# The recurrent block of a hybrid diffusion step: GpSimd's work given to VectorE and ScalarE, layer 0's conditioning given to TensorE

## The chip, the cores and the metric

The kernel runs on one core of a Trainium2 chip. A core has TensorE (matrix products, PE in the profile, its weight loads PEld), VectorE (DVE), ScalarE (ACT), GpSimd (POOL) and a queue for transfers, SyncE (SP). The metric is the device time of one execution in microseconds (us).

## The reference, cut to what matters

1,024 latent tokens and 128 context tokens of width 1024 go through two layers. Layer 0 mixes tokens with a bidirectional RG-LRU, layer 1 with latent attention; each is followed by an MLP with a hidden width of 4096. Every sub-layer is normalised and modulated by six vectors a layer (shift, scale, gate, twice), which come from a conditioning vector, one for the latents and one for the context:

```
mod = silu(cond) @ w_ada + b_ada            # 1024 -> 6 x 1024, for c and c_ctx
sh1, sc1, g1, sh2, sc2, g2 = split(mod, 6)
h = rms_norm(x, g) * (1 + sc1) + sh1
```

The recurrent block of layer 0:

```
xb, yb = split(h @ w_in, 2);  yb = gelu(yb)
xb = depthwise_conv(xb, conv_w, conv_b)     # four taps along the tokens
r, i = sigmoid(xb @ wa + ba), sigmoid(xb @ wx + bx)   # 8 blocks of 128, two directions
a = exp(-8 * r * softplus(-lam));  b = sqrt(1 - a*a) * (i * xb)
h_t = a_t * h_(t-1) + b_t                   # forwards and backwards
out = ((h_f + h_b) * yb) @ w_out
x = x + g1 * out
```

## The kernel before

Channels lie on the 128 partitions and tokens along the row, 1,152 in three chunks of 384 (`CH`). Each float32 operand of a large product is split into two parts, hi and lo, and a product is three TensorE instructions (`mm3`, L118: hi hi, hi lo, lo hi), so a group of 8 blocks of k for one output tile and one chunk is 24 instructions into one of eight PSUM banks.

Weights come as a stream of pieces of 128x1024. `prefetch` (L83) loads a piece through SP into one of two `raw` buffers, ScalarE copies it to `whi` (L94) and GpSimd subtracts to get `wlo` (L95). The first 20 pieces (`RG_STREAM`) belong to the recurrent block.

The conditioning is done in two ways. For the first two vectors of layer 0 (j = 0 the shift, j = 1 the scale), `first_half` loads `ada_w0` and multiplies with the conditioning as the stationary operand (L420), which gives rows; the rows are copied and transposed back (L443, L446). The last four tiles of the scale are dot products instead: `ada_dot` (L142) on VectorE for the latents, and for the context a product on GpSimd (L435) that ScalarE sums later. All other tiles are dots: `ada` (L149) loads a 128x1024 tile of the transposed weights into a `raw` buffer and VectorE makes two dots (L144), one for each condition, against `cb`, the activated condition on every partition. Sixteen such tiles are taken during the recurrent block (`ADA_RG`), eight in its output projection, and the others in the MLP of layer 0.

After the norm of chunk 0 the first group makes x channels 0 and 1 and y channel 0 together for all chunks. Then `rglru` (L510) goes through n = 0 to 7 in the order `RG_ORDER`: the products of x channel n+1 (`xb`, L603), two or more chunks of y products (drained through Gelu, L599), and `gates(n)` (L540). ScalarE copies x out of PSUM (`copy_raw`, L516). `conv` (L519) makes the first tap with bias on GpSimd (L522) and adds three taps on VectorE, each in two segments (L529, six instructions). `conv_split` splits it (L138 on ScalarE, L139 on VectorE). `gates` does 36 products, twelve tanh passes (L554), exp (L563), tanh (L568), the product (L571), 1-A on GpSimd (L574), square root (L577), two products (L580, L581) and two scans for each direction (L585). GpSimd copies the final state (L589), adds both directions (L590) and multiplies with y (`finish`, L593). Row buffers of 128x1152 come from one pool of twelve (`unit`, L507); `raw_x` and `xf` of the convolution, `xfh`, `xfl`, `tr`, `ti`, `A` are all of it. At the end `hs` is split into `zhi`, `zlo`, and `rg_out` (L655) loads `cb` again from a copy in DRAM and starts the output projection.

The order on each engine is written by a scheduler from the program's order, and within an engine it is kept.

Of the kernel before, what the change touches and what calls it, by code (L numbers as in the profile page):

```python
# [15 lines left out]
D = 1024  # L16
# [35 lines left out]
ADA_ORDER = [(0, 2), (0, 3), (0, 4), (0, 5)] + [(1, _j) for _j in range(6)]  # L52

ADA_RG = (2, 2, 2, 2, 2, 2, 2, 2)


class Emit:
# [25 lines left out]
    def prefetch(self, upto):  # L83
# [3 lines left out]
        while self.piece_i < min(upto, self.I["wts"].shape[0]):  # L87
# [7 lines left out]
            nc.gpsimd.tensor_tensor(out=lo, in0=raw, in1=hi.bitcast(F32), op=ALU.subtract)  # L95
# [66 lines left out]
    def mod_finish(self, l, j, conds=(0, 1)):  # L162
# [100 lines left out]
    def group(self, items, rhs, drain, after=None, chunks=range(NCH)):  # L263
        """items: (m, piece index, [block of k]); rhs(k, c): (hi, lo)."""
# [72 lines left out]
    def run(self, stop=99):  # L337
        nc, tc, I, O = self.nc, self.tc, self.I, self.O
        with (
# [12 lines left out]
            self.one_row = const.tile([1, 128], F32, name="one_row")  # L352
            nc.vector.memset(self.one_row, 1.0)
# [5 lines left out]
            self.cb_d = nc.dram_tensor("cb_d", [1, 2, 1024], F32).ap()  # L359
# [13 lines left out]
    def make_cb(self, pool):  # L373
        nc = self.nc
        self.cb = pool.tile([128, 2, 1024], F32, name="cb")
        for i in range(2):
            row = self.wp.tile([128, 1024], F32, tag="raw", name="raw", bufs=2)[0:1]
            nc.sync.dma_start(row, self.I["crow"][:, i])
            for j in range(2):
                ps = self.bank(512)  # L380
                nc.tensor.matmul(
                    ps, lhsT=self.one_row, rhs=row[:, j * 512:(j + 1) * 512], start=True, stop=True
                )
                nc.scalar.activation(out=self.cb[:, i, j * 512:(j + 1) * 512], in_=ps, func=AF.Silu)

    def first_half(self, stop):
        nc, tc, I = self.nc, self.tc, self.I
        cbp = self.alloc(name="cb", bufs=1, side="right")
        rgt = self.alloc(name="rgt", bufs=1, side="right")
        self.cells = None  # L390
        self.junk = rgt.tile([128, 1024], mybir.dt.bfloat16, name="junk")
        self.rgt = rgt
        cs = self.rgt.tile([128, 2, 8], F32, name="cs")
        nc.scalar.activation(out=cs, in_=self.v("cond", 0, 16), func=AF.Silu)
        self.make_cb(cbp)
# [17 lines left out]
        row = [self.bank(512) for _ in range(3)]  # L413
        for k in range(8):
            if k % 2 == 0:
                w2 = self.cpool.tile([128, 2, 3, 512], F32, tag="C", name="ada0")
            w = w2[:, k % 2]
            nc.sync.dma_start(w, I["ada_w0"][k * 128:(k + 1) * 128].rearrange("p (i n) -> p i n", i=3))
            for i in range(3):
                nc.tensor.matmul(  # L420
                    row[i][0:2], lhsT=cs[:, :, k], rhs=w[:, i], start=(k == 0), stop=(k == 7)
                )
# [18 lines left out]
        for i in range(3):  # L441
            srow = self.unit("srow")[0:2, :512]
            tc.keep_in_program_order(nc.scalar.copy(out=srow, in_=row[i][0:2]))  # L443
            for k in range(4):
                o = 2 * (4 * i + k)
                nc.tensor.transpose(psm[:, o:o + 2], srow[:, k * 128:(k + 1) * 128], self.ident[0:2, 0:2])  # L446
        psm = psm.rearrange("p (k t) -> p t k", t=2)
# [62 lines left out]
    def rglru(self, H, gens):  # L510
# [97 lines left out]
        for n in range(2):  # L608
            raws[n] = self.unit("raw_x")
# [614 lines left out]
```

## Time and profile before

| | |
|---|---|
| time, median of 3 runs | 2902.98 us (2900.94 to 2904.37) |
| span of the profiled execution | 2905.1 us |
| TensorE busy | 2744.2 us, 94% of the span, 16,031 instructions |
| VectorE busy | 1483.3 us, 51% |
| ScalarE busy | 1142.5 us, 39% |
| GpSimd busy | 694.9 us, 24%, 337 instructions |
| mean granted TensorE clock | 0.969 |

The span runs from the first to the last instruction of one execution; no time of its own is listed for that execution beyond it, and the span is 2.1 us above the median of the runs. "Busy" is the time in which an engine works on an instruction. Idle time before an instruction is put down to what released it, after an arrow. The granted clock is TensorE's, as a share of 2.4 GHz; its two levels are 2.4 and 1.2 GHz, so 0.86 is a mean over time at both.

### The profile page before, as it was taken

The numbers are of one execution on the slowest core, as the hardware profiler recorded it, in microseconds if no ns is written. First come the engines' busy times: TensorE is split into PE (matmuls) and PEld (weight loads), VectorE is DVE, ScalarE is ACT, GpSimd is POOL, SyncE is SP. The second block draws the span as 40 slices with busy tenths as digits, with TensorE's granted clock in tenths as the row PEclk, the third lists the DMA queues.
The fourth block names the chain that finished last, engine by engine and source line by source line (L and its number), as shares of the span: only waits on it lengthen the run. The fifth ranks groups of instructions, "written<-read, shape, count | busy, mean of one in ns | idle before, by whom it ended". The sixth has DMA issues, their size and how long they took to land. (4 is left out here: it accounts for less than half of the span.)

```text
span 2905.1 us, 39768 instructions
## 1 busy us (share of the span) xinstructions
PE 2744.2 (94%) x16031; PEld 2700.1 (93%) x16031; DVE 1483.3 (51%) x2805; ACT 1142.5 (39%) x2174; POOL 694.9 (24%) x337
## 2 busy tenths in 40 slices
PE   7878679899999999998997999999999999999998
PEld 4878669899999999998997999999999999999998
DVE  7799986844354435326364666662732222223225
ACT  4555551422312322233334877872423222312332
POOL 4276662221211112122142000001211121212121
PEclk8989879999999999999998999999999999999999
DMA  5111114122222223112146211225011010101111
GB/s 220 44 58 59 58 51 174 58 95 80 80 95 70 97 67 106 61 59 102 40 131 224 77 55 56 75 75 191 30 37 51 30 59 30 59 30 51 37 43 67
DMA packets 78608, 223.89 MB, mean 77 GB/s; under 512 B 7764, under 2 KB 36244, under 8 KB 76758
## 3 DMA queue, kind: packets, MB, share of 16 engines
q1 hardware_dynamic: 77654, 218.19, 22.0%
q0 software_dynamic: 768, 3.15, 0.3%
q8 instruction: 126, 2.06, 0.3%
q14 instruction: 60, 0.48, 0.1%
HBM read 185.48 MB, written 33.21 MB: 75 GB/s over the span
## 5 line engine op out<-in xcount | busy, mean ns | idle before, releaser
L95 POOL TENSOR_TENSOR wlo<-raw,whi 128x1024 fp32r<-128x1024 f32 x181 | 454.2, 2510 | 1766.6 <-ACT whi L94 1742.3
L120 PE MATMUL ps<-hhi,whi 128*128 128x384 f32 x2088 | 706.4, 340 | 13.4 <-ACT hhi L247 9.5
L124 PE MATMUL ps<-hhi,wlo 128*128 128x384 f32 x2088 | 706.5, 339 | 4.1 <-POOL wlo L95 4.1
L123 PE MATMUL ps<-hlo,whi 128*128 128x384 f32 x2088 | 707.0, 339 | 0.0
L94 ACT CAST whi<-raw 128x1024 fp32r<-128x1024 f32 x181 | 190.3, 1052 | 868.7 <-PE ps L123 692.4
L120 PE MATMUL ps<-hid,whi 128*128 128x384 f32 x1536 | 516.2, 336 | 0.0
L123 PE MATMUL ps<-hid,whi 128*128 128x384 f32 x1536 | 515.5, 336 | 0.0
L124 PE MATMUL ps<-hid,wlo 128*128 128x384 f32 x1536 | 515.4, 336 | 0.0
L257 DVE SCALAR_TENSOR_TENSOR X<-ps,mod,X 128x256 f32<-128x256 f32 (+1 forms) x576 | 279.9, 514 | 446.2 <-PE ps L124 418.4
L120 PEld LDWEIGHTS ps<-hhi,whi 128*128 128x128 f32 x2088 | 397.7, 191 | 14.0 <-ACT hhi L247 9.6
L124 PEld LDWEIGHTS ps<-hhi,wlo 128*128 128x128 f32 x2088 | 397.7, 191 | 4.9 <-POOL wlo L95 4.9
L123 PEld LDWEIGHTS ps<-hlo,whi 128*128 128x128 f32 x2088 | 398.0, 191 | 0.5 <-DVE hlo L248 0.4
L139 DVE TENSOR_TENSOR hid<-cell,hid 128x384 fp32r<-128x384 f32 x192 | 138.8, 730 | 464.6 <-ACT hid L138 464.5
L120 PEld LDWEIGHTS ps<-hid,whi 128*128 128x128 f32 x1536 | 288.8, 188 | 0.0
L123 PEld LDWEIGHTS ps<-hid,whi 128*128 128x128 f32 x1536 | 288.7, 188 | 0.0
L124 PEld LDWEIGHTS ps<-hid,wlo 128*128 128x128 f32 x1536 | 288.7, 188 | 0.0
L144 DVE SCALAR_TENSOR_TENSOR junk<-raw,cb 128x1024 bf16<-128x1024 f32 x80 | 123.9, 1549 | 181.2 <-DMA raw<-ada_wt 172.1
L312 ACT ACTIVATE cell<-ps 128x384 f32<-128x384 f32 x192 | 93.6, 488 | 296.6 <-PE ps L124 296.4
L947 ACT ACTIVATE p<-ps,nm 128x384 f32<-128x384 f32 (+1 forms) x200 | 112.9, 576 | 39.9 <-DVE nm L942 39.8
L139 DVE TENSOR_TENSOR pt<-ps,pt 128x384 fp32r<-128x384 f32 (+1 forms) x200 | 106.5, 543 | 37.1 <-ACT pt L138 36.8
L932 DVE TENSOR_REDUCE mx<-ps 128x1 f32<-128x384 f32 (+1 forms) x200 | 108.0, 540 | 27.2 <-PE ps L931 26.5
L187 POOL TENSOR_TENSOR acc<-acc,cell 128x384 f32<-128x384 f32 x48 | 53.1, 1105 | 222.8 <-ACT cell L185 185.5
(188 smaller groups left out, 4327.0 us busy)
## 6 DMA issues: line engine op xcount, KB each, us to landing
raw<-wts SPq DMA_DIRECT2D x181, 512.0 KB, 3.7
raw<-ada_wt SPq DMA_DIRECT2D x80, 512.0 KB, 3.7
qn_d<-qn SPq DMA_DIRECT2D x12, 768.0 KB, 5.7
q<-qn_d SPq DMA_DIRECT2D x16, 576.0 KB, 4.5
o_d<-o SPq DMA_DIRECT2D x64, 128.0 KB, 1.7
ada<-ada_w SPq DMA_DIRECT2D x8, 768.0 KB, 12.1
x<-xt SPq DMA_DIRECT2D x3, 1536.0 KB, 10.8
X<-xt SPq DMA_DIRECT2D x3, 1536.0 KB, 11.2
```

Of the source, the lines that this page charges most:

```text
L94: nc.scalar.copy(out=hi, in_=raw)
L95: nc.gpsimd.tensor_tensor(out=lo, in0=raw, in1=hi.bitcast(F32), op=ALU.subtract)
L120: mm = nc.tensor.matmul(ps, lhsT=w[0], rhs=h[0], start=first, stop=False)
L123: nc.tensor.matmul(ps, lhsT=w[0], rhs=h[1], start=False, stop=False)
L124: nc.tensor.matmul(ps, lhsT=w[1], rhs=h[0], start=False, stop=last)
L139: (lo_eng or nc.vector).tensor_tensor(out=lo, in0=src, in1=hi.bitcast(F32), op=ALU.subtract)
L144: self.nc.vector.scalar_tensor_tensor(out=w if cond else self.junk, in0=w, scalar=1.0, in1=self.cb[:, cond], op0=ALU.mult, op1=ALU.mult, a ...
L187: eng.tensor_tensor(out=st[key], in0=st[key], in1=s, op=ALU.add)
L257: self.nc.vector.scalar_tensor_tensor(out=self.X[c][:, m, a:b], in0=ps[:, a:b], scalar=self.mod[:, l, j, cond, m:m + 1], in1=self.X[c][:, ...
L312: nc.scalar.activation(out=r, in_=ps, func=AF.Relu)
L932: nc.vector.tensor_reduce(out=mx[:, j:j + 1], in_=ps, axis=AX.X, op=ALU.max)
L947: nc.scalar.activation(out=p[:, j * CH:j * CH + w], in_=ps, func=AF.Exp, scale=SCALE, bias=nm[:, 1:2], accum_out=sm[:, j:j + 1],)
```

## The change

Layer 0's shifts, scales and gate j = 0 to 4 become products with the weight tile as the stationary operand and the two conditions as two columns (`ada_mm`: eight products of 128x128 by 2 a tile, the sum over k in one bank). Shift and scale (16 tiles) are done at the start, from row buffers; j = 2, 3, 4 (24 tiles) in the recurrent block, three tiles after each n, from two buffers of their own (`ada_pe`). The dots on VectorE in the block and at the start go; those of j = 5 and of layer 1 stay and begin with the output projection. The first tap of the convolution is a second ScalarE pass out of PSUM. The weight splits of the block's pieces, 1-A, the final states, the sum of the scans and the products with y go from GpSimd to VectorE. GpSimd keeps half of the squares' sums for the norms (L187) and the weight splits behind the block. `cb` is loaded at the block's end from the raw condition and activated there. In the diff, parts are left out at lines of three dots; lines in which only a comment goes are not shown.

```diff
-ADA_ORDER = [(0, 2), (0, 3), (0, 4), (0, 5)] + [(1, _j) for _j in range(6)]
-
-ADA_RG = (2, 2, 2, 2, 2, 2, 2, 2)
+ADA_ORDER = [(0, 5)] + [(1, _j) for _j in range(6)]
+ADA_PE = [(_j, _k) for _j in (2, 3, 4) for _k in range(8)]
...
             nc.scalar.copy(out=hi, in_=raw)
-            nc.gpsimd.tensor_tensor(out=lo, in0=raw, in1=hi.bitcast(F32), op=ALU.subtract)
+            eng = nc.vector if self.piece_i < len(RG_STREAM) else nc.gpsimd
+            eng.tensor_tensor(out=lo, in0=raw, in1=hi.bitcast(F32), op=ALU.subtract)
...
-    def mod_finish(self, l, j, conds=(0, 1)):
+    def ada_mm(self, ps, w, k, first, last):
+
+        for f in range(8):
+            self.nc.tensor.matmul(
+                ps[:, 2 * f:2 * f + 2], lhsT=w[:, f * 128:(f + 1) * 128], rhs=self.cs[:, :, k],
+                start=first and f == 0, stop=last and f == 7,
+            )
+
+    def ada_pe(self, n):
+        for j, k in self.pe_jobs[:n]:
+            w = self.rgt.tile([128, 1024], F32, tag="adaw", name="adaw", bufs=2)
+            self.nc.sync.dma_start(w, self.I["ada_n"][j, k * 128:(k + 1) * 128])
+            if k == 0:
+                self.ada_ps = self.bank(16)
+            self.ada_mm(self.ada_ps, w, k, k == 0, k == 7)
+            if k == 7:
+                self.mod_finish(0, j, self.ada_ps)
+        del self.pe_jobs[:n]
+
+    def mod_finish(self, l, j, ps=None):
         nc = self.nc
         o = VEC["ada_b"][0] + (l * 6 + j) * 8
         b = self.vec[:, o:o + 8]
-        for cond in conds:
+        for cond in range(2):
             m = self.mod[:, l, j, cond]
-            nc.vector.tensor_tensor(out=m, in0=m, in1=b, op=ALU.add)
+            src = m if ps is None else ps.rearrange("p (k t) -> p t k", t=2)[:, cond]
+            nc.vector.tensor_tensor(out=m, in0=src, in1=b, op=ALU.add)
...
-    def make_cb(self, pool):
...
-        cbp = self.alloc(name="cb", bufs=1, side="right")
-        rgt = self.alloc(name="rgt", bufs=1, side="right")
+        self.rgt = self.alloc(name="rgt", bufs=1, side="right")
         self.cells = None
-        self.junk = rgt.tile([128, 1024], mybir.dt.bfloat16, name="junk")
-        self.rgt = rgt
-        cs = self.rgt.tile([128, 2, 8], F32, name="cs")
-        nc.scalar.activation(out=cs, in_=self.v("cond", 0, 16), func=AF.Silu)
-        self.make_cb(cbp)
+        self.pe_jobs = list(ADA_PE)
+        self.cs = self.rgt.tile([128, 2, 8], F32, name="cs")
+        nc.scalar.activation(out=self.cs, in_=self.v("cond", 0, 16), func=AF.Silu)
...
-        row = [self.bank(512) for _ in range(3)]
+        ps = [self.bank(16) for _ in range(2)]
         for k in range(8):
-            if k % 2 == 0:
-                w2 = self.cpool.tile([128, 2, 3, 512], F32, tag="C", name="ada0")
-            w = w2[:, k % 2]
-            nc.sync.dma_start(w, I["ada_w0"][k * 128:(k + 1) * 128].rearrange("p (i n) -> p i n", i=3))
-            for i in range(3):
-                nc.tensor.matmul(
-                    row[i][0:2], lhsT=cs[:, :, k], rhs=w[:, i], start=(k == 0), stop=(k == 7)
-                )
+            for j in (1, 0):
+                w = self.unit("ada")[:, :1024]
+                nc.sync.dma_start(w, I["ada_n"][j, k * 128:(k + 1) * 128])
+                self.ada_mm(ps[j], w, k, k == 0, k == 7)
             if k == 2:
                 y = self.rstd(sts[0], D)
             if k == 4:
                 r = self.spread(y)
...
-        ws = []
-        for k in range(4, 8):
-            if k in (4, 7):
-                w3 = self.cpool.tile([128, 3, 1024], F32, tag="C", name="ada1")
-            w = w3[:, (k - 4) % 3]
-            nc.sync.dma_start(w, I["ada_wt"][0, (8 + k) * 128:(9 + k) * 128])
-            self.ada_dot(w, 0, 1, k, 0)
-            nc.gpsimd.tensor_tensor(out=w, in0=w, in1=self.cb[:, 1], op=ALU.mult)
-            ws.append(w)
         load_x0(1)
         load_x0(2)
-        nc.sync.dma_start(self.cb_d, self.cb[0:1])
-        psm = self.bank(24)
...
-        self.mod_finish(0, 1, [0])
-        self.mod_finish(0, 0)
+        self.mod_finish(0, 1, ps[1])
+        self.mod_finish(0, 0, ps[0])
         hpair()
...
-                out=self.junk, in_=ws[k - 4], func=AF.Copy, accum_out=self.mod[:, 0, 1, 1, k:k + 1]
-            ))
-        self.mod_finish(0, 1, [1])
...
-            nc.scalar.copy(out=raws[n][:, c * CH:(c + 1) * CH], in_=ps)
+            cs = slice(c * CH, (c + 1) * CH)
+            raw, xf = raws[n]
+            nc.scalar.copy(out=raw[:, cs], in_=ps)
+            nc.scalar.activation(
+                out=xf[:, cs], in_=ps, func=AF.Identity, scale=self.v("conv_w", 8 + n), bias=self.v("conv_b", n)
+            )
 
         def conv(n):
-            raw, xf = raws.pop(n), self.unit("xf")
+            raw, xf = raws.pop(n)
             cw = lambda k: self.v("conv_w", k * 8 + n)
-            nc.gpsimd.tensor_scalar(
-                out=xf, in0=raw, scalar1=cw(1), scalar2=self.v("conv_b", n), op0=ALU.mult, op1=ALU.add
-            )
...
-                nc.gpsimd.tensor_scalar(
+                nc.vector.tensor_scalar(
...
-                nc.gpsimd.tensor_copy(out=self.fin[:, d, n:n + 1], in_=u[:, e:e + 1])
-            nc.gpsimd.tensor_tensor(out=tr[0], in0=tr[0], in1=tr[1], op=ALU.add)
+                nc.vector.tensor_copy(out=self.fin[:, d, n:n + 1], in_=u[:, e:e + 1])
+            nc.vector.tensor_tensor(out=tr[0], in0=tr[0], in1=tr[1], op=ALU.add)
...
-            raws[n] = self.unit("raw_x")
+            raws[n] = self.unit("raw_x"), self.unit("xf")
...
-                    finish(m, j, nc.gpsimd)
+                    finish(m, j, nc.vector)
                     have.remove((m, j))
-                self.ada(ADA_RG[n])
+                self.ada_pe(3)
...
-        nc.sync.dma_start(self.cb, self.cb_d.to_broadcast([128, 2, 1024]))
+        nc.sync.dma_start(self.cb, I["crow"].to_broadcast([128, 2, 1024]))
+        nc.scalar.activation(out=self.cb, in_=self.cb, func=AF.Silu)
...
-        "ada_w0": np.ascontiguousarray(a["ada_w"][0, :, :D + 512]),
+        "ada_n": np.ascontiguousarray(a["ada_w"][0, :, :5 * D].reshape(D, 5, D).transpose(1, 0, 2)),
```

## Rows read from the trace of the kernel before

**Rows 1.** The page's first line: the span.

```profile
span 2905.1 us, 39768 instructions
```

**Rows 2.** Windows: length, busy us and instruction count of each engine, granted clock, DMA.

```profile
100.00:440.00 340.00, 260.33 (x1330) 253.00 (x1329) 312.02 (x250) 191.36 (x259) 210.26 (x86) 0.86 0.19 63
...
148.00:380.00 232.00, 178.47 (x911) 174.48 (x910) 226.38 (x166) 135.01 (x177) 156.40 (x66) 0.86 0.17 57
...
600.00:640.00 40.00, 40.00 (x231) 40.00 (x231) 18.67 (x37) 3.16 (x3) 6.15 (x3) 1.00 0.21 73
```

**Rows 3.** Timeline of VectorE in 100 to 440: start, length, instruction, idle before.

```profile
109.86 1.21 DVE L144 SCALAR_TENSOR_TENSOR junk<-raw,cb 128x1024 bf16<-128x1024 f32 x1
...
112.33 1.35 DVE L139 TENSOR_TENSOR xfl<-xf,xfh 128x1152 fp32r<-128x1152 f32 x1
...
113.60 4.45 DVE L529 SCALAR_TENSOR_TENSOR xf<-raw_x,vec,xf 128x1023 f32<-128x1023 f32 x6
...
145.63 2.32 DVE L585 TENSOR_TENSOR_SCAN tr<-A,vec,ti 128x1024 f32<-128x1024 f32 x1
...
148.19 11.22 DVE L529 SCALAR_TENSOR_TENSOR xf<-raw_x,vec,xf 128x1023 f32<-128x1023 f32 x6
...
222.94 11.27 DVE L529 SCALAR_TENSOR_TENSOR xf<-raw_x,vec,xf 128x1023 f32<-128x1023 f32 x6
...
284.35 2.62 DVE L571 SCALAR_TENSOR_TENSOR A<-A,tr 128x1152 f32<-128x1152 f32 x2
...
379.98 1.33 DVE L564 SCALAR_TENSOR_TENSOR ti<-ti,xf 128x1152 f32<-128x1152 f32 x1
...
400.43 0.15 DVE L168 TENSOR_TENSOR mod<-mod,vec 128x8 f32<-128x8 f32 x1
...
426.31 1.02 DVE L594 TENSOR_TENSOR hs<-hs,tr 128x384 f32<-128x384 f32 x2
```

**Rows 4.** Timeline of GpSimd in 100 to 260.

```profile
131.68 3.25 POOL L574 TENSOR_SCALAR A<-A 128x1152 f32<-128x1152 f32 x2 [21.88 <-DVE A L571]
...
229.18 4.88 POOL L594 TENSOR_TENSOR hs<-hs,tr 128x384 f32<-128x384 f32 x3
```

**Rows 5.** ScalarE by line and shape, 110 to 420: busy us, mean ns.

```profile
L517 ACT COPY raw_x<-ps 128x384 f32<-128x384 f32 x18 | 7.7, 476 | 0.0
```

**Rows 6.** Timeline of the start, all engines.

```profile
19.88 1.50 PE L195 MATMUL ps<-ones,acc 128*128 128x2 f32 x12
...
31.84 12.18 POOL L435 TENSOR_TENSOR ada<-ada,cb 128x1024 f32<-128x1024 f32 x4
...
36.28 3.23 DVE L144 SCALAR_TENSOR_TENSOR junk<-ada,cb 128x1024 bf16<-128x1024 f32 x1
...
45.47 1.01 PE L120 MATMUL ps<-hhi,whi 128*128 128x384 f32 x2 [9.49 <-ACT hhi L247]
```

**Rows 7.** Window 20 to 30, columns as above.

```profile
20.00:30.00 10.00, 10.00 (x34) 3.12 (x35) 4.23 (x15) 2.09 (x2) 3.75 (x2) 1.00 1.02 411
```

**Rows 8.** Waits in 110 to 420: us in total, times, longest.

```profile
ACT ti L554 <- DVE tr L585: 30.2, 5, 8.3
...
DVE junk L144 <- DMA raw<-ada_wt: 10.6, 3, 5.8
...
SPq L153 <- POOL wlo L95: 123.6, 12, 15.5
```

**Rows 9.** Timeline of VectorE, GpSimd and TensorE at the block's end.

```profile
393.16 1.23 DVE L144 SCALAR_TENSOR_TENSOR junk<-raw,cb 128x1024 bf16<-128x1024 f32 x1 [5.80 <-DMA raw<-ada_wt]
...
410.71 9.12 DVE L139 TENSOR_TENSOR zlo<-hs,zhi 128x384 fp32r<-128x384 f32 x5
...
413.35 2.96 POOL L590 TENSOR_TENSOR tr<-tr 128x1152 f32<-128x1152 f32 x1
...
413.40 0.69 PE L123 MATMUL ps<-zlo,whi 128*128 128x384 f32 x1 [12.33 <-DVE zlo L139]
```

**Rows 10.** The page's DMA issues: KB each, us from issue to landing.

```profile
raw<-ada_wt SPq DMA_DIRECT2D x80, 512.0 KB, 3.7
```

More of the change, by code (lines that the diff above doesn't have):

```diff
@@ L351, in run @@
             nc.vector.memset(self.ones, 1.0)
-            self.one_row = const.tile([1, 128], F32, name="one_row")
-            nc.vector.memset(self.one_row, 1.0)
             self.mod = const.tile([128, 2, 6, 2, 8], F32, name="mod")
@@ L358, in run @@
             self.qp_d = nc.dram_tensor("qp_d", [HEADS, 128, T], F32).ap()
-            self.cb_d = nc.dram_tensor("cb_d", [1, 2, 1024], F32).ap()
             cp = self.alloc(name="cpool", bufs=9)
@@ L371, in v @@
         return self.vec[:, o:o + n]
-    def make_cb(self, pool):
[L374 to L380, printed above, removed]
-                nc.tensor.matmul(
-                    ps, lhsT=self.one_row, rhs=row[:, j * 512:(j + 1) * 512], start=True, stop=True
-                )
-                nc.scalar.activation(out=self.cb[:, i, j * 512:(j + 1) * 512], in_=ps, func=AF.Silu)
     def first_half(self, stop):
         nc, tc, I = self.nc, self.tc, self.I
-        cbp = self.alloc(name="cb", bufs=1, side="right")
-        rgt = self.alloc(name="rgt", bufs=1, side="right")
+        self.rgt = self.alloc(name="rgt", bufs=1, side="right")
         self.cells = None
-        self.junk = rgt.tile([128, 1024], mybir.dt.bfloat16, name="junk")
-        self.rgt = rgt
-        cs = self.rgt.tile([128, 2, 8], F32, name="cs")
-        nc.scalar.activation(out=cs, in_=self.v("cond", 0, 16), func=AF.Silu)
-        self.make_cb(cbp)
+        self.pe_jobs = list(ADA_PE)
+        self.cs = self.rgt.tile([128, 2, 8], F32, name="cs")
+        nc.scalar.activation(out=self.cs, in_=self.v("cond", 0, 16), func=AF.Silu)
         xs, sts = [], [{} for _ in range(NCH)]
@@ L427, in first_half @@
         self.prefetch(2)
-        ws = []
-        for k in range(4, 8):
-            if k in (4, 7):
-                w3 = self.cpool.tile([128, 3, 1024], F32, tag="C", name="ada1")
-            w = w3[:, (k - 4) % 3]
-            nc.sync.dma_start(w, I["ada_wt"][0, (8 + k) * 128:(9 + k) * 128])
-            self.ada_dot(w, 0, 1, k, 0)
-            nc.gpsimd.tensor_tensor(out=w, in0=w, in1=self.cb[:, 1], op=ALU.mult)
-            ws.append(w)
         load_x0(1)
         load_x0(2)
-        nc.sync.dma_start(self.cb_d, self.cb[0:1])
-        psm = self.bank(24)
[L441 to L447, printed above, removed]
-        for j, ks in ((1, slice(0, 4)), (0, slice(0, 8))):
-            for cond in range(2):
-                tc.keep_in_program_order(nc.vector.tensor_copy(
-                    out=self.mod[:, 0, j, cond, ks], in_=psm[:, cond, 8 * j:8 * j + ks.stop]
-                ))
-        self.mod_finish(0, 1, [0])
-        self.mod_finish(0, 0)
+        self.mod_finish(0, 1, ps[1])
+        self.mod_finish(0, 0, ps[0])
         hpair()
@@ L461, in first_half @@
         square(1, range(4, 8))
-        for k in range(4, 8):
-            tc.keep_in_program_order(nc.scalar.activation(
-                out=self.junk, in_=ws[k - 4], func=AF.Copy, accum_out=self.mod[:, 0, 1, 1, k:k + 1]
-            ))
-        self.mod_finish(0, 1, [1])
         square(2)
@@ L516, in copy_raw @@
         def copy_raw(n, c, ps):
-            nc.scalar.copy(out=raws[n][:, c * CH:(c + 1) * CH], in_=ps)
+            cs = slice(c * CH, (c + 1) * CH)
[4 more added lines that the diff above has]
+            )
         def conv(n):
-            raw, xf = raws.pop(n), self.unit("xf")
+            raw, xf = raws.pop(n)
             cw = lambda k: self.v("conv_w", k * 8 + n)
-            nc.gpsimd.tensor_scalar(
-                out=xf, in0=raw, scalar1=cw(1), scalar2=self.v("conv_b", n), op0=ALU.mult, op1=ALU.add
-            )
             for k in (0, 2, 3):
@@ L608, in rglru @@
         for n in range(2):
-            raws[n] = self.unit("raw_x")
+            raws[n] = self.unit("raw_x"), self.unit("xf")
         for c in range(NCH):
```

1 line of the change is left out of this document (removed).

## Prediction

> **What bounds the kernel now.** I read the granted clock and busy shares by stretch first, then VectorE and GpSimd row by row in the stretch the change touches, then the start, the end of that stretch, and who waits for a DMA. The profiled execution spans 2905.1 us [rows 1], 2.1 us (0.07%) above the median of the runs, 2902.98, and they spread over 3.4 us; I do the sum against the span and take 2 off at the end. A change within 0.2% (6 us) can't be told from none.
>
> From about 440 us on, TensorE is the bound: in 600 to 640 it is busy for all 40.00 us at full granted clock and starts 231 products, 40/231 = 0.173 us each [rows 2]. The change does next to nothing to that part. In 100 to 440, the recurrent block after its first group, TensorE is another thing: 260 of 340 us busy at a clock of 0.86 [rows 2]. The code issues 1224 products of 384 columns there (six x pieces of 72, 504 for y, 288 for the gates): 1224 x 0.173 = 212 us. So 128 us of this stretch are waits and the half clock that follows waits. In the six regular periods (148 to 380) VectorE is busy for 226.4 of 232 us: it is the bound there, with GpSimd at 156.4, ScalarE at 135.0 [rows 2].
>
> Why VectorE is full is in its rows [rows 3]. The six shifted multiply-adds of one convolution take 4.45 us at 113.60, and the same six take 11.27 us at 222.94. GpSimd stood idle for 21.88 us before 131.68, so during the short one; during the long one it worked without a pause (229.18 is one of five such rows) [rows 4]. Two A products (L571) take 2.62 us at 284.35, in a pause of GpSimd. At the start one dot of L144 takes 3.23 us beside GpSimd's product of L435 against 1.21 at 109.86 [rows 3, 6]. So the two engines hold each other up, and the undisturbed price of a VectorE pass over 128x1152 is half of 2.62 less overlap, 1.27 us (start to start, 112.33 to 113.60).
>
> One period is the time from one convolution to the next. From 148.19 to 379.98 there are six: 231.8/6 = 38.6 us [rows 3]. At undisturbed prices VectorE's work in one is: convolution 4.4, split 1.27, eight passes of the gate arithmetic 10.2, two scans (145.63 to 148.19: 2.56 each) 5.1, four conditioning dots (1.21 each, with read-out) 4.9. Sum 25.9, where it was busy 226.4/6 = 37.7. About 11.8 us a period go to GpSimd's presence.
>
> **The change part by part.**
>
> *Work onto VectorE, per period.* Two passes 1-A: VectorE has no such long row with one input. Bounds: a small instruction, 0.15 (L168 at 400.43), and a pass of the same width with two inputs, 1.27; it is nearest to the latter in size, and I use that: 2.5 us. The sum of the two scans 1.27. Three products with y of 128x384, 0.47 each (two in 1.02 at 426.31 [rows 3]): 1.4. Two one-column copies at the small instruction's 0.15: 0.3. Weight splits: 20 pieces in 8 periods, 2.5 at 1.14 (a 128x1024 two-input pass, 1.21 less the overlap): 2.9. Together 8.4. The four dots (4.9) go. VectorE then has 25.9 - 4.9 + 8.4 = 29.4 us, 27.2 with the lower end, and GpSimd does nothing in the steady part.
>
> The Trainium skill, VectorE: DVE Perf Modes, section "The perf-mode tier table", gives a float32 tensor_scalar between SBUF tiles twice the rate of a two-input pass (1227 against 2293 ns at 2048 columns). No run here shows it yet; by it the 1-A passes are an estimated 0.7 us each and VectorE's period 28.2.
>
> *Onto ScalarE.* The first tap of the convolution becomes three ScalarE passes of 128x384 out of PSUM a period, like L517 at 0.476 [rows 5]: 135.0/6 + 1.4 = 23.9 us. It lies beside TensorE, but ScalarE empties the banks in order.
>
> *Onto TensorE.* A period has 72 products for x, 48 for y, 36 for gates: 156 x 0.173 = 27.0. Three conditioning tiles of eight products with two columns add 24. Nearest row: the two-column float32 products of L195, twelve in 1.50 us [rows 6], 0.125 each: 3.0. At half clock I bound it by double, 6.0; nothing is free below. Period 30.0 us (33.0).
>
> So TensorE needs 30.0, VectorE 29.4, ScalarE 23.9, in place of 38.6 set by VectorE. They are tied to each other through the twelve row buffers of the block (a gate's tanh waits for a scan to free one: 30.2 us in five waits [rows 8]), and the raw and xf buffers of a convolution are now taken together, one earlier. I take 34: 4 us of the present 11.6 of TensorE's waiting stay. Gain 6 x 4.6 = **28**. Ends: 31 (46) and 37 (10).
>
> *Start.* The first product now starts at 45.47 [rows 6], because the last conditioning tiles are reduced on VectorE and GpSimd at 3.2 us each. After, all tiles of shift and scale are products. DMA: x of 1536 KB and 16 tiles of 512 KB are 9.96 MB, with vectors 10.2 MB; at 411 GB/s [rows 7] 24.8 us, and with issue and landing about 27.5. Eight products 1.0, six small VectorE steps 1.2, scale and shift 1.2: 30.9; two weight pieces land by 30.1 and are split by 32.3. The sixteen tiles take row buffers that the squares use too, so some DMA waits: I say 33.5, gain **12**. Ends: 14, or 5 if the 128 products run at half clock (128 x 0.25 = 32 us from 6 on).
>
> *First convolutions.* GpSimd's xf pass in front of convolution 0 and its stretch go. Of TensorE's loss in 100 to 120 I take back **5**; ends 0 and 8.
>
> *End of the block.* Three things stand behind the last gates: VectorE waits 5.80 us for a conditioning tile's DMA with the A products queued behind the dot (393.16); five z splits take 9.12 (410.71) in place of 5 x 0.47 = 2.4; GpSimd's sum of the scans ends at 413.35 + 2.96 = 416.3 in place of 412.0. TensorE waits 12.33 us there [rows 9]. The first is 5.8; the other two overlap to about 6. Against them: the condition row is now loaded raw and passed through Silu by ScalarE at the block's end, and the splits of the output projection's weights stay on GpSimd; 2. Gain **10**, ends 4 and 14.
>
> *What the tiles cost TensorE by waiting.* Its queue is in order, so a late tile holds products and the bank drains behind them. VectorE waited 10.6 us for sixteen such tiles [rows 8]; for 24, 16 us, but they have two buffers of their own now rather than the weights'. I put a quarter here: **-4**, ends 0 and -16.
>
> Conditioning of layer 0's j = 5 and layer 1 goes on as before under a busy TensorE: 0.
>
> Sum: 12 + 5 + 28 + 10 - 4 = 51. 2905 - 51 = 2854, less 2 for the runs: **2852 us**.
>
> **The rivals.**
>
> *All of it.* TensorE becomes the full bound: periods of 31 (46), start 14, convolutions 8, end 13, no waits: 81, **2822 us**. For it: TensorE has most work in the period. Against it: VectorE is 0.6 us behind. 12 in 100.
>
> *The ring of row buffers holds.* Gates, exp, tanh, square root, products and scans of one n must end before the next n gets buffers, and ScalarE's order doesn't change. Periods of 37, with end 5: 10 + 12 + 5 + 5 - 2 = 30, **2873 us** (up to 2890 with a colder start). For it the 30.2 us of waits on scans; against it that these scans are stretched now. 17 in 100.
>
> *Not the presence of GpSimd but the work itself.* If VectorE's passes keep their present lengths, a period is 37.7 - 4.9 + 8.4 = 41.2, 2.6 longer: +16, against -12 at the start and -6 at the end: **2901 us**, no change. The 4.45 against 11.27 speaks against it. 4 in 100. Here the Trainium skill, Perfetto Trace Analysis, section "Optimizing Scalar/DVE Operations", speaks against the change: where VectorE is saturated, work should go from it to ScalarE or even GpSimd. The same section warns that these two share a read port, so that moving work between them may not help; the trace here bears out the warning.
>
> *Slower.* TensorE waits for each of the 24 tiles. A 512 KB tile lands 3.7 us after issue [rows 10]; issued only when SP's queue gets past weight loads that wait for a split, it costs the whole landing: 24 x 3.7 = 89 against 55 gained: +34, **2937 us**. It decides from 55/24 = 2.3 us a tile. For it: SP stood 123.6 us in twelve waits of a conditioning load for a weight split [rows 8]. Against it: VectorE had to wait for three tiles in sixteen only, and the tiles get their own buffers. 7 in 100.
>
> **How the numbers follow.** The forecast with its bounds (gain 36 to 70) has 60 in 100, all of it 12, the ring 17, no shrinking 4, slower 7. The predicted time is the forecast's. The range from 2818 to 2886 leaves out the slower case, no change, and the far ends: about 15 to 20 in 100. Faster by more than 0.2%: 0.60 + 0.12 + 0.17 = 0.89; same 0.04; slower 0.07.
>
> **What would show it.** First product at 31 to 36 us. The six-step convolution at about 4.5 us everywhere, scans of 2.3 us, no GpSimd row from the steady part. Periods of 33 to 35 us and TensorE's clock above 0.92 there. The out-projection's first products some 50 us earlier. The prediction is wrong if VectorE's passes stay long, if TensorE's waits name the tile loads, or if the periods stay above 36 with VectorE idle, waiting for ScalarE.

## Result and the profile after

| | before | after |
|---|---|---|
| median of 4 runs, us | 2901.96 (2900.61 to 2904.37) | 2882.43 (2879.69 to 2883.34) |
| ratio, 95% interval | | 0.9928 [0.9914, 0.9942] |
| profiled span, us | 2905.1 | 2881.6 |

The change gains about 20 us, where 51 were forecast. In the page of the kernel after, the span and the busy times of the engines:

```profile
span 2881.6 us, 40800 instructions
...
PE 2801.2 (97%) x16603; PEld 2785.6 (97%) x16603; DVE 1387.2 (48%) x2774; ACT 1152.8 (40%) x2185; POOL 474.5 (16%) x247
```

I read the stretches first, against [rows 2]. Windows of the kernel after (length; busy us and count of TensorE, its weight loads, VectorE, ScalarE, GpSimd; granted clock; DMA):

```profile
30.00:70.00 40.00, 40.00 (x189) 40.00 (x189) 0.00 (x0) 0.00 (x0) 0.00 (x0) 1.00 0.36 133
75.00:140.00 65.00, 61.05 (x332) 58.80 (x332) 51.30 (x109) 39.66 (x78) 7.09 (x6) 0.97 0.10 33
140.00:400.00 260.00, 260.00 (x1526) 259.85 (x1524) 208.91 (x218) 190.35 (x255) 5.28 (x2) 0.92 0.22 76
162.97:373.83 210.86, 210.86 (x1226) 210.73 (x1225) 168.70 (x181) 149.06 (x199) 0.00 (x0) 0.90 0.24 81
168.00:172.00 4.00, 4.00 (x37) 4.00 (x36) 4.00 (x6) 3.97 (x8) 0.00 (x0) 1.00 0.22 65
170.00:180.00 10.00, 10.00 (x54) 10.00 (x53) 7.67 (x7) 7.92 (x8) 0.00 (x0) 0.62 0.43 130
174.00:182.00 8.00, 8.00 (x37) 8.00 (x36) 3.67 (x3) 3.95 (x4) 0.00 (x0) 0.50 0.42 129
600.00:640.00 40.00, 40.00 (x232) 40.00 (x231) 19.81 (x36) 7.17 (x10) 9.58 (x4) 1.00 0.23 79
```

In 30 to 70 TensorE works alone: no other compute engine does anything. In the block (140 to 400) it is busy for all 260 us and VectorE for 209: the bound has passed from VectorE to TensorE. GpSimd is nearly silent (5 us). The clock is 0.92 although TensorE never pauses.

The start and one piece of the block, in TensorE's timeline of the kernel after (start, length, instruction, idle before):

```profile
16.10 6.96 PE L165 MATMUL ps<-cs,ada 128*128 128x2 f32 x32 [16.10 <-DMA ada<-ada_n]
22.92 2.70 PE L215 MATMUL ps<-ones,acc 128*128 128x2 f32 x12
...
29.57 44.37 PE L165 MATMUL ps<-cs,ada 128*128 128x2 f32 x208
74.85 1.01 PE L120 MATMUL ps<-hhi,whi 128*128 128x384 f32 x2 [0.91 <-ACT hhi L267]
...
168.07 0.34 PE L124 MATMUL ps<-xfh,wlo 128*128 128x384 f32 x1
168.24 3.63 PE L165 MATMUL ps<-cs,adaw 128*128 128x2 f32 x32
171.73 0.42 PE L120 MATMUL ps<-hhi,whi 128*128 128x384 f32 x1
...
172.62 0.52 PE L120 MATMUL ps<-hhi,whi 128*128 128x384 f32 x1
...
174.53 6.82 PE L165 MATMUL ps<-cs,adaw 128*128 128x2 f32 x32
181.22 0.67 PE L124 MATMUL ps<-hhi,wlo 128*128 128x384 f32 x1
...
404.32 0.55 PE L123 MATMUL ps<-zlo,whi 128*128 128x384 f32 x1 [3.15 <-DVE zlo L139]
```

The first large product starts at 74.85, where it was at 45.47 [rows 6] and I forecast 33.5. The rows in front of it are the narrow conditioning products, 44.37/208 = 0.213 us each. Before the tiles at 168.24 a large product has 0.34, behind them 0.52.

The same narrow products, grouped by shape over 0 to 560 (count, busy us, mean ns of one):

```profile
L165 PE MATMUL ps<-cs,ada 128*128 128x2 f32 x256 | 54.9, 352 | 16.1 <-DMA ada<-ada_n 16.1
L165 PE MATMUL ps<-cs,adaw 128*128 128x2 f32 x384 | 49.1, 262 | 0.0
```

The code issues 16 x 8 = 128 products at the start and 24 x 8 = 192 in the block; the trace has 256 and 384. A float32 product of this form is two TensorE instructions, each with its load of a 128x128 weight block (the PEld count follows the PE count). The twelve rows of L195 [rows 6], by which I priced a product, were six products too: the code of `rstd` issues three times two.

From start to start, the 32 instructions at 168.24 take (171.73 - 168.24)/32 = 0.109 us each, with the granted clock at 1.00 (168 to 172); the 32 at 174.53 take (181.22 - 174.53)/32 = 0.209, with the clock at 0.50, its lower level of 1.2 GHz (174 to 182). So 0.109 is the price at the upper level and about 0.21 the price at the lower one; the block's mean, 49.1/384 = 0.128, is a mixture of the two.

The granted clock reads 1.00 from 0 to 70, yet an instruction takes 0.213 us there, the price of the lower level. The sums at L215 (L195 before) take 2.70 where they took 1.50 [rows 6]. The window's figure does not show the half rate of this start; the run "warm" below does.

VectorE's timeline of the kernel after, one convolution with its neighbours, and both ends of the six periods (the first step of the convolution that was at 148.19, and the product that was at 379.98), against [rows 3]:

```profile
162.97 1.26 DVE L500 SCALAR_TENSOR_TENSOR xf<-raw_x,vec,xf 128x1023 f32<-128x1023 f32 x1
...
177.98 1.36 DVE L139 TENSOR_TENSOR xfl<-xf,xfh 128x1152 fp32r<-128x1152 f32 x1 [0.92 <-ACT xfh L138]
...
218.53 1.42 DVE L545 TENSOR_SCALAR A<-A 128x1152 f32<-128x1152 f32 x2
...
224.94 2.34 DVE L556 TENSOR_TENSOR_SCAN tr<-A,vec,ti 128x1024 f32<-128x1024 f32 x1
...
232.91 1.02 DVE L565 TENSOR_TENSOR hs<-hs,tr 128x384 f32<-128x384 f32 x2
233.84 3.00 DVE L500 SCALAR_TENSOR_TENSOR xf<-raw_x,vec,xf 128x1023 f32<-128x1023 f32 x4
...
373.83 1.35 DVE L535 SCALAR_TENSOR_TENSOR ti<-ti,xf 128x1152 f32<-128x1152 f32 x1
```

All stand at the undisturbed lengths. Two 1-A passes take 1.42, so 0.71 each; I had used 1.27. The estimate of 0.7 worked out from the Trainium skill, VectorE: DVE Perf Modes, section "The perf-mode tier table", agrees.

The end of the same stretch on TensorE: one product that waits for the same weight split of GpSimd in both kernels, before and after.

```profile
433.37 0.44 PE L124 MATMUL ps<-zhi,wlo 128*128 128x384 f32 x1 [0.93 <-POOL wlo L95]
...
419.23 0.44 PE L124 MATMUL ps<-zhi,wlo 128*128 128x384 f32 x1 [0.86 <-POOL wlo L95]
```

### The profile page after: what moved, and what is told of

It reads as the page before. It is cut to its first block, busy times and chain, and to the rows that moved or that the text cites. A ratio compares the mean times of both kernels' runs of the same rounds, so it can differ in the third digit from the quotient of the medians.

```text
span 2881.6 us, 40800 instructions
## 1 busy us (share of the span) xinstructions
PE 2801.2 (97%) x16603; PEld 2785.6 (97%) x16603; DVE 1387.2 (48%) x2774; ACT 1152.8 (40%) x2185; POOL 474.5 (16%) x247
## 3 DMA queue, kind: packets, MB, share of 16 engines
q0 software_dynamic: 768, 3.15, 0.3%
## 5 line engine op out<-in xcount | busy, mean ns | idle before, releaser
L95 POOL TENSOR_TENSOR wlo<-raw,whi 128x1024 fp32r<-128x1024 f32 x161 | 388.5, 2413 | 2035.4 <-ACT whi L93 2035.4
L144 DVE SCALAR_TENSOR_TENSOR junk<-raw,cb 128x1024 bf16<-128x1024 f32 x56 | 97.7, 1745 | 106.4 <-DMA raw<-ada_wt 103.9
L267 ACT ACTIVATE hhi<-cell,mod 128x384 fp32r<-128x384 f32 (+2 forms) x128 | 64.5, 533 | 101.7 <-DVE mod L188 60.4
## 6 DMA issues: line engine op xcount, KB each, us to landing
ada<-ada_n SPq DMA_DIRECT2D x16, 512.0 KB, 10.2
```

What stands on the lines that cost most here:

```text
L95: eng.tensor_tensor(out=lo, in0=raw, in1=hi.bitcast(F32), op=ALU.subtract)
L144: self.nc.vector.scalar_tensor_tensor(out=w if cond else self.junk, in0=w, scalar=1.0, in1=self.cb[:, cond], op0=ALU.mult, op1=ALU.mult, a ...
L267: nc.scalar.activation(out=hi, in_=t, func=AF.Identity, bias=sh, scale=1.0)
```

## Experiments

Each time is a median with its runs, each ratio is to the kernel before, timed in the same batch (2902.1 to 2903.4 us).

### Which half of the change pays: one part alone

**elem_only**: the kernel before, with only the elementwise work and the weight splits moved; conditioning stays as it was.

```diff
-            nc.gpsimd.tensor_tensor(out=lo, in0=raw, in1=hi.bitcast(F32), op=ALU.subtract)
+            eng = nc.vector if self.piece_i < len(RG_STREAM) else nc.gpsimd
+            eng.tensor_tensor(out=lo, in0=raw, in1=hi.bitcast(F32), op=ALU.subtract)
...
-                nc.gpsimd.tensor_scalar(
+                nc.vector.tensor_scalar(
                     out=A[d], in0=A[d], scalar1=-1.0, scalar2=1.0, op0=ALU.mult, op1=ALU.add
```

> The kernel before with only the elementwise work and the weight splits moved off GpSimd; the conditioning as before (rows and dots, the dots on VectorE in the block). Theory (GpSimd's presence stretched VectorE): VectorE needs about 33 to 34 us a period in place of 38.6, end of block 10 earlier, the whole 2855 to 2868, faster than the changed kernel. Rival (the block gained because the dots left VectorE): 2890 or more.

2854.84 us (2854.47 to 2856.14), 0.9836 [0.982, 0.985]: a gain of 48 by this half alone, more than by the whole change.

**cond_only**: the kernel after with the elementwise work and splits given back to GpSimd.

```diff
-                nc.vector.tensor_scalar(
+                nc.gpsimd.tensor_scalar(
                     out=A[d], in0=A[d], scalar1=-1.0, scalar2=1.0, op0=ALU.mult, op1=ALU.add
```

> The changed kernel with the elementwise work and the weight splits put back on GpSimd, so only the conditioning differs from before. If the two parts simply add (elementwise alone took 48 us off, both together 20): 2903 + 28 = 2931. Theory (start 29 later, but VectorE, stretched by GpSimd and the bound of the block, loses dots that take it 2.9 us a tile, 46 in all, until TensorE binds at about 35 us a period): 2900 to 2912.

2895.64 us (2890.71 to 2898.81), 0.9977 [0.9968, 0.9987]: it gains 7 where I expected no change or a loss. The four corners are 2903 (neither), 2855 (elementwise), 2896 (conditioning), 2882 (both): the halves don't add. Conditioning on TensorE gains 7 while GpSimd works and costs 28 once it doesn't. TensorE's first large product of cond_only and of elem_only:

```profile
75.01 1.01 PE L119 MATMUL ps<-hhi,whi 128*128 128x384 f32 x2 [0.91 <-ACT hhi L266]
...
43.60 1.01 PE L121 MATMUL ps<-hhi,whi 128*128 128x384 f32 x2 [6.58 <-ACT hhi L248]
```

The start loses some 30 us either way (75.01 against 45.47 [rows 6], 74.85 against 43.60). So the 28 lie at the start. Behind it conditioning on TensorE gains 7 + 30 = 37 us while GpSimd works, and 31.3 - 27.6, some 4, once it doesn't. The block's windows of the two show why. First elem_only:

```profile
140.00:400.00 260.00, 215.53 (x1155) 210.67 (x1156) 237.96 (x289) 168.12 (x232) 24.94 (x5) 0.91 0.26 90
```

and cond_only:

```profile
140.00:400.00 260.00, 257.71 (x1501) 256.75 (x1502) 225.91 (x150) 176.39 (x225) 156.26 (x76) 0.92 0.22 76
```

With conditioning on TensorE, TensorE is full (258 of 260) even beside a busy GpSimd, so what is then taken from GpSimd gains only 13 (2895.64 to 2882.43). With it on VectorE, VectorE is the fullest and TensorE has 44 us to spare; the longest of TensorE's waits there, 24.4 us in three, are for ScalarE's copies of weights.

### The start

**start_few**: of the start's products only the first of each tile is issued, and for the last tile of each of the two vectors all eight; all loads stay, so scale and shift of the first norm are partial sums.

```diff
-        for f in range(8):
+        for f in range(8 if last or self.rgt_run else 1):
```

> The changed kernel with most narrow products of the start left out: of each tile of shift and scale the first of its eight, all eight only for the last tile of each j, so shift and scale hold the wrong sums; every load stays. Theory (the prediction failed at the price of these products alone, its 33.5 us for the loads was right): 60 instructions, 13 us, first large product at 32 to 38 us in place of 74.85, the whole 2840 to 2848. Rival (loads through the twelve row buffers, which SP took until 33 us to issue, set a floor too): 45 or later, the whole 2853 or more.

TensorE's timeline of start_few:

```profile
32.48 0.59 PE L166 MATMUL ps<-cs,ada 128*128 128x2 f32 x2 [0.69 <-DMA ada<-ada_n]
33.76 6.99 PE L166 MATMUL ps<-cs,ada 128*128 128x2 f32 x32 [0.69 <-DMA ada<-ada_n]
41.66 1.01 PE L121 MATMUL ps<-hhi,whi 128*128 128x384 f32 x2 [0.91 <-ACT hhi L268]
```

2846.21 us (2845.26 to 2848.58), 0.9806 [0.979, 0.982], 36 below after. The first product lies between my two expectations. The tiles land every 1.28 us, the last but one is there at 33.8 and so the last at about 35; the 32 instructions of these two make up most of the rest up to 41.66. I had all loads landed at 27.5, some 7 us too early: SP issues the second chunk of x and two weight pieces, 2.6 MB, ahead of the tiles (x at 3.08, the tiles from 3.94), and my sum of 10.2 MB left them out. But 33 us of the delay (74.85 - 41.66) are the products'.

**start_rows**: the same sums with the two condition columns stationary and the tile moving, 2 x 512 columns, as the kernel before does it at L420; then row copies and transposes.

```diff
-                self.ada_mm(ps[j], w, k, k == 0, k == 7)
+                for i in range(2):
+                    nc.tensor.matmul(
+                        row[j][i][0:2], lhsT=self.cs[:, :, k], rhs=w[:, i * 512:(i + 1) * 512],
+                        start=(k == 0), stop=(k == 7),
+                    )
...
+                tc.keep_in_program_order(nc.scalar.copy(out=srow, in_=row[j][i][0:2]))
+                for k in range(4):
...
+                    nc.tensor.transpose(psm[:, o:o + 2], srow[:, k * 128:(k + 1) * 128], self.ident[0:2, 0:2])
```

> The changed kernel with the 16 tiles of shift and scale multiplied the other way round: the two conditions stationary, the tile moving in two products of 512 columns, the rows then copied and transposed; no GpSimd in it. Theory (the 256 narrow TensorE instructions of 0.21 us between 16 and 74 us are the start): 64 instructions at 0.43 to 0.85, first large product at 43 to 48 us in place of 74.85, the whole about 2854. Rival (the tiles are late, since they pass through twelve row buffers: SP took 29 us to issue them): first product after 60, the whole above 2868.

TensorE's timeline of start_rows, its first rows of either kind:

```profile
16.11 12.71 PE L420 MATMUL ps<-ada,cs 128*2 128x512 f32 x24 [16.11 <-DMA ada<-ada_n]
...
51.01 0.71 PE L120 MATMUL ps<-hhi,whi 128*128 128x384 f32 x2 [1.26 <-ACT hhi L267]
```

2857.5 us (2854.3 to 2861.68), 0.9845 [0.983, 0.986]: 25 below after, and the first product 24 earlier. Four instructions a tile at 12.71/24 = 0.53 us cost 2.1 us, sixteen narrow ones 3.4. Behind the first six tiles they cost less, 10.46/24 = 0.44 (24 of them at 37.61), and the sums at L215 take 1.50 again, as in the kernel before. What the start loses comes back one to one.

**warm**: the kernel after with products of 512 columns between the tiles (eight ahead, one behind each; nothing reads them), to try whether the narrow products are slow only because TensorE is at its lower clock.

```diff
+        self.wide(8)
...
                 self.ada_mm(ps[j], w, k, k == 0, k == 7)
+                self.wide(1)
```

> The changed kernel with products of 512 columns into an unused bank: eight ahead of the first tile, one after each of the 16 tiles. Theory (the narrow products run at half clock because nothing wide ran before them): 0.13 us an instruction in place of 0.21, 16 x (2.1 + 0.9) = 47 us, first large product at 62 to 66 in place of 74.85, the whole about 2872. Rival (0.21 is set by something else at the start, the loads beside them or the row buffers): first product at 85 to 90, the whole about 2896.

2907.51 us (2899.88 to 2913.95), 1.0014 [1.000, 1.003]: a miss. TensorE's timeline of warm:

```profile
16.26 2.14 PE L165 MATMUL ps<-cs,ada 128*128 128x2 f32 x16 [3.77 <-DMA ada<-ada_n]
18.26 2.05 PE L173 MATMUL ps<-wsrc,ident 128*128 128x512 f32 x2
20.11 3.41 PE L165 MATMUL ps<-cs,ada 128*128 128x2 f32 x16
...
99.33 1.63 PE L120 MATMUL ps<-hhi,whi 128*128 128x384 f32 x2
```

and its window:

```profile
20.00:40.00 20.00, 20.00 (x77) 16.79 (x76) 1.62 (x10) 0.00 (x0) 0.00 (x0) 0.50 0.67 256
```

After the eight wide products the first tile's sixteen instructions take 2.14 us. By the second tile the granted clock is at the lower of its levels (0.50, 1.2 GHz) and the same sixteen take 3.41, as in the kernel after. It stays there up to the first large product, with TensorE busy all the time and a wide product after each tile: one wide product a tile did not hold it. So the 16 us that I had for the start's products become 28 by the second instruction of each (256 x 0.109) and 54.9 by the lower clock. TensorE had waited 3.77 us before that first tile, so this run alone does not tell the wait from the narrow products. The kernel after does: over 140 to 400 TensorE never waits, and yet the clock falls to 0.50 behind six of its runs of narrow products, as at 172 above (the runs at 168, 209, 237, 275, 311 and 359). Other runs are not followed by a fall: those in 140 to 150 and 341 to 350, and short ones at 248, 286 and 319.

### The block

**block_none**: the kernel after without the 24 tiles' loads and products in the block; the three conditioning vectors are then their biases alone.

```diff
-            w = self.rgt.tile([128, 1024], F32, tag="adaw", name="adaw", bufs=2)
-            self.nc.sync.dma_start(w, self.I["ada_n"][j, k * 128:(k + 1) * 128])
...
-            self.ada_mm(self.ada_ps, w, k, k == 0, k == 7)
```

> The changed kernel without the 24 tiles of j = 2, 3, 4 in the recurrent block: their loads and products are left out and these three vectors are the biases alone. Theory (TensorE is the bound of the block, with 49 us of narrow instructions and some 13 us of half clock after them): the block is shorter by 40 to 60, the whole 2825 to 2842, and VectorE, 209 of 260 us busy now, nearly full. Rival (the ring of row buffers and VectorE are right behind, TensorE's products only fill waits): 2867 or more.

2851.1 us (2848.76 to 2852.55), 0.9821 [0.981, 0.984]: 31 below after, less than expected. Its window:

```profile
140.00:400.00 260.00, 235.68 (x1293) 231.54 (x1292) 230.43 (x251) 201.03 (x273) 15.03 (x5) 0.95 0.17 61
```

TensorE and VectorE are now level, and TensorE waits for weight splits (15.4 us in five waits). Under the products lies VectorE as next bound, so not all of their 49 us and of the clock's loss comes back.

**spread**: the kernel after with the block's narrow products put singly between large ones in place of 24 in a row.

```diff
                     self.mm3(ps, self.blk(p, b), rhs(k, c), k == 0, k == len(blocks) - 1)
+                    if self.spreading and k % 5 in (0, 2, 4):
+                        self.ada_step()
```

> The changed kernel with the 192 narrow products of the block put singly between the wide ones, three after every eight blocks of k or so, in place of three tiles together after each n. Theory (it is the narrow products standing together that let the clock fall, to 0.62 to 0.83 in ten windows of 10 us): 384 instructions at 0.128, no half clock, 10 to 14 us less, about 2870. Rival (the clock falls for other reasons, or the narrow ones cost the same anywhere): 2879 or more.

2875.77 us (2873.15 to 2880.15), 0.9914 [0.990, 0.993]: 7 below after, between my two expectations. The granted clock over 140 to 400 is 0.93, after 0.92, and in 170 to 190 still 0.74. The order gives little back, against the 31 us for leaving the products out (block_none).

**wide_block**: start_rows with the wide form in the block too (the loop of start_rows put into the function for the block's tiles).

```diff
-            self.ada_mm(self.ada_ps, w, k, k == 0, k == 7)
+            for i in range(2):
+                nc.tensor.matmul(
+                    self.ada_rows[i][0:2], lhsT=self.cs[:, :, k], rhs=w[:, i * 512:(i + 1) * 512],
```

> The kernel of start_rows with the 24 tiles of the block multiplied the wide way too, in place of 16 narrow instructions a tile four of 512 columns; rows copied and transposed at the end of each j; two banks held. Theory: 96 x 0.43 = 41 us in place of 49 and no half clock after them (13), so 12 to 20 less than start_rows, until VectorE binds: 2838 to 2846. Rival (banks held and VectorE behind): 2855 or more.

2875.13 us (2874.15 to 2877.31), 0.9911 [0.990, 0.993]: a miss, 18 above start_rows. TensorE's waits in 100 to 440 (us in total, times, longest) name what I had not priced, the transposes that stand in its queue behind ScalarE's row copies:

```profile
PE ps L189 <- ACT srow L186: 19.6, 2, 11.1
```

**wide_late**: the same with the transposes one group later; the copied rows now take one of the tiles' two buffers.

```diff
+        self.ada_late()
         for j, k in self.pe_jobs[:n]:
```

> The kernel of wide_block with the transposes of each j's rows put after the next n, so that TensorE does not stand behind ScalarE's row copies (19.6 us in two waits). Theory (the wide form is the cheaper one and only these waits made wide_block slow): 12 to 20 less than start_rows, 2838 to 2846. Rival (the two banks that the rows hold all through the block are the price): 2860 or more.

2863.84 us (2861.78 to 2866.11), 0.9866 [0.985, 0.988]: the wait for ScalarE is gone and 11 us with it, but it is still 6 above start_rows, a miss again. TensorE now waits for the tile that was put behind the row buffer:

```profile
PE ps L189 <- DMA adaw<-ada_n: 15.2, 6, 8.5
```

Beside that wait 96 wide instructions cost some 48 us, as much as the 384 narrow ones. In the block, where TensorE is the bound, no form of these products was free. What the two banks cost that the rows hold was not tried.

### Is GpSimd's presence the cause?

**pool_back**: block_none with 60 GpSimd passes over 128x1024 in the block whose result nobody reads. TensorE, VectorE and ScalarE have the same work as in block_none.

```diff
+                for _ in range(10 if n < 6 else 0):
+                    nc.gpsimd.tensor_tensor(
+                        out=self.scr, in0=self.scr, in1=self.fin[:, 0, n:n + 1].to_broadcast([128, 1024]), op=ALU.mult
+                    )
```

> The kernel of block_none (no tiles of j = 2, 3, 4) with work for GpSimd that nobody waits for: after each n from 0 to 5 ten products of a scratch tile of 128x1024 with a final state, about 26 us a period, as much as GpSimd had before. VectorE's own work is that of block_none. Theory (GpSimd's presence stretches VectorE's passes by some 11.8 us a period): 70 us, less the 20 to 30 that VectorE has free: 2885 to 2920. Rival (VectorE was slow for its own work, and engines side by side don't touch): 2845 to 2858.

2937.82 us (2937.19 to 2939.12), 1.0121 [1.011, 1.014]: 87 above block_none, more than expected. Its timeline, GpSimd first:

```profile
203.90 25.86 POOL L616 TENSOR_TENSOR scr<-scr,fin 128x1024 f32<-128x1024 f32 x10 [17.74 <-DVE fin L559]
...
218.32 4.88 DVE L564 TENSOR_TENSOR hs<-hs,tr 128x384 f32<-128x384 f32 x3
223.13 7.97 DVE L499 SCALAR_TENSOR_TENSOR xf<-raw_x,vec,xf 128x1023 f32<-128x1023 f32 x4
231.02 2.61 DVE L534 SCALAR_TENSOR_TENSOR ti<-ti,xf 128x1152 f32<-128x1152 f32 x2
```

and its window:

```profile
140.00:400.00 260.00, 164.46 (x887) 162.55 (x886) 254.62 (x170) 141.11 (x184) 143.28 (x58) 0.81 0.07 23
```

Beside the passes three products with y take 4.88 us (1.49 in after, at 205.16), and the convolution's four steps, of which the last are free again, 7.97 (3.00); at 231.02, with GpSimd done, two passes take 2.61. VectorE is the bound at once. TensorE waits 82.9 us for splits in six waits, where it waited 15.4 in block_none: 67 of the 87. Its granted clock is 0.81 there, 0.95 in block_none. The Trainium skill, SBUF — State Buffer, section "Who interferes with whom", says that a VectorE instruction with two SBUF inputs contends with a GpSimd instruction that reads SBUF; these rows agree.

### A version of both

**mix**: elem_only with one of the three vectors in the wide form on TensorE, a tile per n; one as dots on VectorE, a tile per n; the third as dots in the output projection.

```diff
-ADA_ORDER = [(0, 2), (0, 3), (0, 4), (0, 5)] + [(1, _j) for _j in range(6)]
+ADA_ORDER = [(0, 3), (0, 4), (0, 5)] + [(1, _j) for _j in range(6)]
...
-ADA_RG = (2, 2, 2, 2, 2, 2, 2, 2)
+ADA_RG = (1, 1, 1, 1, 1, 1, 1, 1)
...
+                self.ada_pe(1)
                 self.ada(ADA_RG[n])
```

> The kernel of elem_only with the block's conditioning divided: j = 2 on TensorE the wide way, one tile after each n, j = 3 as dots on VectorE, one tile after each n, j = 4 as dots in the output projection as before. Theory (VectorE is the bound of elem_only's block with 33 us a period): 2.4 us less a period, TensorE 28.8, the whole 2836 to 2846. Rival (what TensorE waits for in elem_only is ScalarE's copies of weights, 24 us in three waits, since tiles and weights share two buffers): 2851 or more.

2845.91 us (2845.65 to 2852.25), 0.9817 [0.980, 0.984]: the fastest complete kernel here, 57 below before and 36 below after. Its window:

```profile
140.00:400.00 260.00, 231.59 (x1219) 214.57 (x1220) 223.91 (x269) 172.46 (x237) 19.82 (x5) 0.94 0.26 92
```

TensorE and VectorE are near level at 232 and 224.

**mix2**: mix with no dots in the block; all sixteen tiles in the first half of the output projection.

```diff
-ADA_RG = (1, 1, 1, 1, 1, 1, 1, 1)
+ADA_RG = (0, 0, 0, 0, 0, 0, 0, 0)
...
-            if l == 0 and m < 4 and c > 0:
-                self.ada(1)
+            if l == 0 and m < 4:
+                self.ada((1, 1, 2)[c])
```

> The kernel of mix without dots in the block: j = 2 on TensorE the wide way, the sixteen tiles of j = 3 and 4 as dots beside the first half of the output projection. Theory (VectorE, 30.8 us a period in mix, falls to 28.3, just under TensorE's 28.8): 2830 to 2842. Rival (sixteen tiles of 2.45 us in 50 us of output projection hold up the residuals there): 2848 or more.

2858.51 us (2857.43 to 2863.28), 0.9853 [0.983, 0.987]: a miss, 13 above mix. Window 400 to 600 of mix2:

```profile
400.00:600.00 200.00, 173.93 (x945) 169.68 (x944) 127.01 (x249) 56.30 (x100) 46.89 (x23) 0.93 0.26 87
```

In mix TensorE is busy 190.3 us there. The projection's first product comes 6 us earlier than in mix (352.94 against 359.11), the sums of the norm behind it 11 us later (474.65 against 464.04). So the projection loses 17; TensorE waits 11.9 us there for ScalarE's copies of weights, in mix not at all.

## Why the prediction was wrong

**The step that failed** is the price of a narrow product, "0.125 each", in "Three conditioning tiles of eight products with two columns add 24", and above all in "Eight products 1.0" at the start, where it let me take the loads for what sets the first product. I took the x12 of L195 [rows 6] for twelve products. They were six, so a product is two instructions: 0.22 us at the upper clock, and 0.43 at the start, which ran at the lower one. The bound "128 x 0.25 = 32" held one of the two factors of two only.

- **Start.** Forecast +12, measured 45.47 - 74.85 = -29, an error of 41 us. The 256 instructions took 54.9 us in place of 16. By start_few 33 us of the error are the products, and most of the rest is the loads, which the sum had some 7 us early. start_rows gives 24 of the 29 back.
- **First convolutions.** Forecast 5. From the first large product to the start of the first regular period it was 148.19 - 45.47 = 102.7 us and is 162.97 - 74.85 = 88.1: gained 15, too small a term. What made it was not taken apart.
- **Six periods.** Forecast from 38.6 to 34. Between the same two steps (379.98 is a product behind the last convolution, not a seventh one) they take (373.83 - 162.97)/6 = 35.1: gained 21 of the 28. VectorE's part was right: its passes have their undisturbed lengths, it is busy 168.7/6 = 28.1 us a period (forecast 29.4) and has slack. TensorE's part came near by another make-up. Forecast were 30.0 of work and 4 of waits. In these 210.9 us TensorE starts 890 large products and 336 narrow instructions, at their full-clock prices 890 x 0.173 + 336 x 0.109 = 191 us, and the granted clock is 0.90, 190 of 210.9: no waits, but dearer work and a lower clock.
- **End of the block.** Forecast 10. From 379.98 to the product at 433.37 it was 53.4 us, from 373.83 to 419.23 it is 45.4: gained 8. TensorE's wait of 12.33 there [rows 9] is 3.15.
- **Sum.** -29.4 + 14.6 + 20.9 + 8.0 = 14.1; the spans differ by 23.5. The other 9 come later: the kernel after is 17 us ahead at the sums of a norm behind the output projection (534.81 against 551.89), 18 at those ahead of layer 1 (1323.01 against 1341.25) and 23 late in layer 1's attention (1939.99 against 1962.88). No run shows why.
- **Waits for tiles.** Put at -4; they were none. Behind the start the terms give 39 and the block gained 43.5, although its products cost double. The slower rival is refuted: no TensorE wait in the block names a tile's load, although SP waited 152.1 us in 21 waits for their two buffers.
- **The ring of row buffers** is refuted: TensorE is never idle, so no chain through the buffers sets the period. Its time, 2873, was nearer than my forecast by a cause that was not there.
- **"Not the presence of GpSimd"** is refuted by elem_only and by pool_back.
- **"All of it"** was right in that TensorE became the full bound, and wrong in that this was a gain: full of what is the question.

What I had not asked is whether the two halves want each other. They don't: the elementwise half alone gains 48, and the conditioning half puts 104 us of narrow products (54.9 + 49.1) on TensorE, which cost 31 at the start and, once GpSimd is silent, gain some 4 behind it.

## What to carry to other kernels

When a change takes the bound off one engine, price what the same change puts on the engine that is bound next, and run the halves apart: here one half alone gains 48 and both gain 20. Before a row's count is used as a price, check it against the code: a count of instructions may be twice the count of products. Small products with a full weight block each cost far more here than their columns say (the list below has the figures). At the start it paid to make the few columns the stationary side (start_rows); in a block where TensorE is the bound neither form was free, so put such work where TensorE has waits.

## What the hardware showed that I had not expected

- A float32 product of a 128x128 block with two columns is two instructions of 0.109 us each at the upper level of the clock (168.24 to 171.73), 0.213 at the lower. With 512 columns it is two of 0.93 in warm (18.26 to 20.11), also at the lower level: 256 times the columns for 4.3 times the time.
- TensorE, busy without a pause, fell to half its clock on narrow products: in the block of after it is granted 1.00 over 168 to 172 and 0.50 over 174 to 182, at 0.109 and 0.209 us an instruction. In warm sixteen of them take 2.14 us, then 3.41 (granted 0.50). What in these products lets it fall was not tried.
- In the first 70 us of the kernel after the window's granted clock reads 1.00, while the instructions take 0.213 us, the length that goes with 0.50 in warm.
- 150 us of GpSimd work that nobody waits for cost 87 us (pool_back against block_none), by stretching VectorE's passes.
